# A decoder layer's merge moved from GpSimd and a shared PSUM bank to VectorE and the score banks, with three edits in its MLP

## The chip, the cores and the metric

The kernel runs on one core of one Trainium2 chip, as one program. The metric is the device time of one execution in microseconds (us); lower is better. Engines: PE (TensorE, matmuls), DVE (VectorE), ACT (ScalarE), POOL (GpSimd), SP (SyncE, which issues the DMAs). Each engine works through its own instructions in a fixed order.

## What is computed

One decoder layer on a prompt of 2048 tokens and a sample of 64 tokens (8 sequences of 8), all in float32:

```python
n = rms_norm(x, ln1_g); proj = n @ w_in                     # 1024 -> 3360 columns
att = dilated_attention(q, k, v, ...)                       # 8 heads x 64, three branches
rw  = rwkv7_time_mix(proj[..., 3 * A_W:], ...)              # recurrent half, 8 heads x 64
h = x + concat([att, rw]) @ w_out
m = rms_norm(h, ln2_g)
y = h + jnp.square(jax.nn.relu(m @ w_mlp1)) @ w_mlp2        # 1024 -> 4096 -> 1024
```

The attention has three branches, (window, dilation) = (128,1), (512,4), (2048,16). Each gives a numerator, a denominator and a row maximum, and the branches are merged with weights `exp(max - max over branches)` over the common denominator. The sample attends to a cache of 2048 keys.

## The kernel before

Products in float32 are split into a high and a low part (`parts` and `split`: ACT writes the high part, DVE or POOL subtracts it to get the low one), and three matmuls high*high, high*low, low*high are summed in PSUM. The program is written as generators; a scheduler that simulates the engines sets the final order on each engine, and memory of a closed pool is taken over by the next pool, whose tiles then wait for the last readers of what lay there.

The stages are, by time: projections and recurrence (0 to 1212 us), prompt attention (1212 to 1790), output projection beside the sample's attention (1790 to 1987), and the MLP (1987 to the end).

**Attention.** `attention(p, ...)` runs head pairs p = 0 to 3. Per pair there are 96 score tiles in three branches b: two matmuls into a score bank of pool `psc` (3 banks, tile `sc`, L1087 and L1088), a bias add with row maximum on DVE (L1090), an exponential on ACT, transposes into `pt` (L1105), and products with the values into `o` (L1112). ACT copies `o` into `ob[b]`. Tile `ob[0]` has two buffers, `ob[1]` and `ob[2]` have one each, so ACT's first copy for branch 1 of pair p+1 waits until pair p is merged. `merge(p, ob, st)` is pumped two steps at a time inside `attention(p+1)`; for p = 3 it runs beside the start of the sample. It makes small products of the maxima and denominators (L1135, L1136, L1144 to L1155), computes the weights on a [128, 128] tile, sends them through memory (`wD`) into the tile `wrow`, and then takes 12 steps, one for each group g of 512 tokens and branch b:

```python
ps = mp()
PE.matmul(ps, wsel[:, g], wr[:, b], start=True, stop=True)
tt(ob[b][:, cs], ps, ob[b][:, cs], ALU.mult)
if b:
    (V if p == 3 else G).tensor_tensor(ob[0][:, cs], ob[0][:, cs], ob[b][:, cs], ALU.add)
```

For p < 3 `mp()` gives the tile `ax` of pool `pax`, which has a single bank. The same bank serves `recurrent_half()`, also pumped inside the attention: 64 groups of 12 matmuls (L1263), each followed by a DVE add `fr`. For p = 3 it gives a score bank.

**MLP.** Three column groups g of 704 columns, 8 rounds r each. A round makes the first product for two blocks f with seven products each (Strassen, `first`, L1628), and then the second product (`second`, L1696) for eight row blocks o; in normal rounds the first part takes 168 matmuls and the second 192. In `second` the weight tile of each o is split by `parts(wr)`, high on ACT and low on DVE (L1571); in `first` products 2 and 6 of the seven have their low part on POOL. In the last round of groups 0 and 1 the generator `normed` builds the seven operand sets of the next group beside `second`: DVE scales (L1493, tile `rl`), POOL makes four sums (L1581 to L1584), ACT and DVE split them (`mh`, `ml`). In the first round of group 0 three operand sets (`quarter`) are still built on DVE and ACT while PE multiplies.

`square_sums` gives the RMS sums of 88 columns: two squares on ACT, three adds on DVE, a matmul with `ones` (L1465). Four of them are left for the end of round 0 of group 0. They read the tile `res1`, which `reload(1)`, at the end of round 1, fills again.

**Memory.** Pool `mw` (weight tiles `wr`, `wh`, `wl`, then `rl` and the squares) is opened after the output projection and starts at byte 110944 of a partition, where pool `wo2` lay: `wr` takes 110944 to 127328, and `wo2`, with the operand tiles `mh` and `ml` of the last projection matmuls, took 110944 to 125024.

Of the kernel before, what the change touches and what calls it, by code (L numbers as in the profile page):

```python
# [9 lines left out]
F32 = mybir.dt.float32  # L10
F32R = mybir.dt.float32r
AF = mybir.ActivationFunctionType
ALU = mybir.AluOpType
# [4 lines left out]
P = 128  # L18
# [12 lines left out]
def bc(ap, axis, n):  # L31
    a = ap.unsqueeze(axis)
    shape = list(a.shape)
    shape[axis] = n
    return a.broadcast_to(shape)
# [136 lines left out]
def _build(ctx, tc, nc, I, O, dbg, upto):  # L172
    V, S, PE, G = nc.vector, nc.scalar, nc.tensor, nc.gpsimd
# [7 lines left out]
    def tt(out, a, b, op):  # L181
        V.tensor_tensor(out, a, b, op)  # L182
# [4 lines left out]
    def pool(**kw):  # L187
        if kw.get("space") is not DRAM:
            kw["reuse_waits"] = "tile"
        return tc.tile_pool(**kw)  # L190
# [6 lines left out]
    ones = const.tile([P, P], F32, name="ones")  # L197
# [791 lines left out]
    psc = ph2.enter_context(pool(name="psc", bufs=3, space=PSUM, side="right"))  # L989
# [137 lines left out]
    def merge(p, ob, st):  # L1127


        def mp():  # L1130
            return psc.tile([P, 512], F32, name="sc") if p == 3 else pax.tile([P, 512], F32, name="ax")

        for ty in range(2):
            for x in range(2):
                G.tensor_tensor(zst[:, x, :, :, 4 * ty:4 * ty + 4], bc(st[:, x, 1, :, ty, :].rearrange("p g q -> p q g"), 3, 4), bc(bc(mk1, 1, 4), 1, 4), ALU.mult)  # L1135
                G.tensor_tensor(mv2[:, ty, x], bc(st[:, x, 2, :, ty, :], 3, 8), bc(bc(rr2, 1, 4), 1, 4), ALU.mult)  # L1136
            yield
        sw = at.tile([P, 6, P], F32, name="sw")
        ps = mp()
# [12 lines left out]
        ps = mp()  # L1152
# [43 lines left out]
        for g in range(4):  # L1196
            cs = slice(g * 512, (g + 1) * 512)
            for b in range(3):
                ps = mp()
                PE.matmul(ps, wsel[:, g], wr[:, b], start=True, stop=True)  # L1200
                tt(ob[b][:, cs], ps, ob[b][:, cs], ALU.mult)
                if b:
                    (V if p == 3 else G).tensor_tensor(ob[0][:, cs], ob[0][:, cs], ob[b][:, cs], ALU.add)
                yield
            nc.sync.dma_start(out=mixA[p, :, cs], in_=ob[0][:, cs])

# [246 lines left out]
    def residual(g):  # L1453
        return hp.tile([P, KT, 2 * HT], F32, name=f"res{g % 2}")

    def square_sums(h, i, c, ps, pl):

        sa = pl.tile([P, 4, SQ], F32, name="sq", tag="mt2", bufs=2)
        sb = pl.tile([P, 4, SQ], F32, name="sq", tag="mt2", bufs=2)
        act(sa, h[:, 0:4, c:c + SQ], AF.Square)  # L1460
        act(sb, h[:, 4:8, c:c + SQ], AF.Square)
        tt(sa, sa, sb, ALU.add)
        tt(sa[:, :2], sa[:, :2], sa[:, 2:], ALU.add)
        tt(sa[:, 0], sa[:, 0], sa[:, 1], ALU.add)
        PE.matmul(ps[:SQ, 0:1], sa[:, 0], ones[:, 0:1], start=True, stop=True)  # L1465
        V.tensor_copy(ssq[i // 8][:SQ, i % 8:i % 8 + 1], ps[:SQ, 0:1])
        if i % 8 == 7:
            q = ssq[i // 8]
            tsc(q, q, 1.0 / D, 1e-6, ALU.mult, ALU.add)
            G.tensor_tensor(rst[i // 8], q, mhalf[:, 0:8], ALU.pow)  # L1470
# [42 lines left out]
    with pool(name="wo2", bufs=1) as wo2, pool(name="pwo", bufs=4, space=PSUM, side="right") as pwo, pool(name="psa", bufs=1, space=PSUM) as psa, pool(name="pst", bufs=1, space=PSUM) as pst:  # L1513
        for k in range(4):
            wo_panel(kqb.tile([P, T], F32R, name="wo", tag="kq"), k)
        for _ in range(2):
            kvt = kqb.tile([P, T], F32, name="kv2", tag="kq")
            kvs += [lambda t=kvt[:, i:i + 1024]: t for i in (0, 1024)]
        sample = sample_all(psa)
        owed = 0  # L1520
        sums0 = sums_first(wo2, lambda: pst.tile([P, 512], F32, name="pst")[:, :HT], m0, rb0)
        for c0 in range(0, NT, NC_):
            if c0 + NC_ == NT:
                for _ in sample:
                    pass
            g, q0 = c0 // (2 * HT), c0 % (2 * HT)
            if q0 == 0:
                res = residual(min(g, 1))
                res0 = res0 if g else res
            h = res[:, :, q0:q0 + NC_]  # L1530
            nc.sync.dma_start(out=h, in_=rD[:, :, c0:c0 + NC_])
            for k in range(4):
                if (k, c0) not in mixed:
                    mixed[k, c0] = mix_panel(*((we, k, c0, 3) if k < 3 else (wo2, k, c0, 2)))
            for o in range(KT):
                ps = pwo.tile([P, 512], F32, name="pwo")
                i = 0
                for k in range(4):
                    mh, ml = mixed[k, c0]
                    for a, b in ((woh, mh), (woh, ml), (wol, mh)):  # L1540
                        PE.matmul(ps[:, :NC_], a[k][:, o * P:(o + 1) * P], b, start=(i == 0), stop=(i == 11))  # L1541
                        i += 1
                tt(h[:, o], ps[:, :NC_], h[:, o], ALU.add)
                if g and o % 4 == 2:
                    next(sums0, None)
                owed += 8
                while owed >= 5:
                    owed -= 5
                    next(sample, None)
            if g:  # L1550
                nc.sync.dma_start(out=hD[:, :, c0:c0 + NC_], in_=h)
            if c0 + NC_ < NT:
                for i in range(NC_ // SQ):
                    square_sums(h, c0 // SQ + i, i * SQ, pst.tile([P, 512], F32, name="pst"), wo2)
    ph3.close()
    mw = ph4.enter_context(pool(name="mw", bufs=2))


# [3 lines left out]
    with pool(name="mm", bufs=1, side="right") as mm, pool(name="pm", bufs=8, space=PSUM) as pm:  # L1562
# [21 lines left out]
            E.tensor_tensor(S[3], B21, S[1], ALU.subtract)  # L1584

        def tmp():
            return mw.tile([P, HT], F32, name="rl", bufs=12)

        def reload(g):
            h = residual(g)  # L1590
# [3 lines left out]
        def normed(g, h, mb):  # L1594

            mb += [operand(i, hp if i in EARLY else mm) for i in range(7)]
            rb = scales(g, mw, bank)
            yield
            for k in range(4):
                B11, B12, B21, B22 = (scaled(V, h, rb, k, x, c, tmp()) for x in range(2) for c in range(2))  # L1600
                S = [tmp() for _ in range(4)]
                sums_b(G, S, B11, B12, B21, B22)
                for i, t in enumerate((B11, B21, B22, *S)):
                    split(t, mb[i][0][:, k], mb[i][1][:, k])
                    if i == 2:
                        yield
                yield
# [76 lines left out]
        def second(r, hs, h, last, base, beside):  # L1684

            for o in range(KT):
                wr = mw.tile([P, 4, P], F32, name="wr", tag="wr", bufs=8)
                nc.sync.dma_start(out=wr, in_=I["w2"][r, o])
                wh, wl = parts(wr)
                for c in range(2):  # L1690
                    ps = bank()
                    cs = slice(c * HT, (c + 1) * HT)
# [11 lines left out]
        for g in range(3):  # L1704
            late = []
            nh = None
            for r in range(8):
# [11 lines left out]
                beside = normed(g + 1, nh, mb2) if last and g < 2 else iter(())  # L1719
                second(r, hs, h, last, g * 2 * HT, beside)  # L1720
                if g == 0 and r == 0:
                    for i in range(20, 24):
                        square_sums(res, i, (i - 16) * SQ, pm.tile([P, 512], F32, name="pm"), mw)
                if g < 2 and r == 1:
                    nh = reload(g + 1)
                for _ in beside:
                    pass
# [37 lines left out]
```

## Time and profile before

| what | us |
|---|---|
| median of 3 runs | 3433.43 |
| lowest, highest run | 3427.34, 3434.07 |
| the profiled execution, its own time | 3430.08 |
| its span, first to last instruction | 3428.3 |
| PE busy | 3165.2 (92%) |
| DVE busy | 2171.6 (63%) |
| ACT busy | 1465.3 (43%) |
| POOL busy | 1071.6 (31%) |
| mean granted clock of PE | 0.955 |

Busy time counts an engine's instructions; PE can be busy at half its clock. Idle time of the other engines costs nothing unless PE waits for them. The device time holds 1.8 us beside the span.

### The profile page before, as it was taken

How to read it: one execution, taken by the hardware profiler on the slowest of the kernel's cores; microseconds unless marked ns; L12 is line 12 of the kernel's file. 1: busy time of each engine (PE TensorE's matmuls, PEld its weight loads, DVE VectorE, ACT ScalarE, POOL GpSimd, SP SyncE). 2: the span in 40 equal slices, each digit the busy share in tenths (PEclk: the TensorE clock that was granted, in tenths of full speed). 3: DMA queues.
4: the chain of work that ended last, by engine and by line, in shares of the span. 5: the costliest groups of instructions: out<-in, count | busy, mean ns of one | idle time of the engine just before them, and what ended most of it. 6: DMA issues, size and time to landing. Idle time of an engine off the chain costs nothing.

```text
span 3428.3 us, 64759 instructions
## 1 busy us (share of the span) xinstructions
PE 3165.2 (92%) x24406; PEld 2883.9 (84%) x24406; DVE 2171.6 (63%) x4576; ACT 1465.3 (43%) x3468; POOL 1071.6 (31%) x1311
## 2 busy tenths in 40 slices
PE   5999999989988889897989789999999999999999
PEld 5877867887887878686868579999999999899999
DVE  4656686776675444353556666767776666967675
ACT  4555565555454356262532333323333333423232
POOL 1004431343044111323210133333543333534342
PEclk9999999999998999897989889999999999999999
DMA  5465575465455575343457722222232222322122
GB/s 165 136 193 153 132 202 151 115 164 161 129 152 134 162 230 170 93 153 98 113 198 262 288 82 93 87 62 87 70 128 71 75 74 75 105 62 87 62 87 71
DMA packets 374493, 439.73 MB, mean 128 GB/s; under 512 B 120067, under 2 KB 236734, under 8 KB 374180
## 3 DMA queue, kind: packets, MB, share of 16 engines
q1 hardware_dynamic: 374180, 435.59, 42.4%
q8 instruction: 192, 3.15, 0.4%
q14 instruction: 121, 0.99, 0.1%
HBM read 338.07 MB, written 102.11 MB: 128 GB/s over the span
## 4 chain that ended last, share of the span: by engine, by line
PE 71%; DVE 11%; DMA 9%; issue 3%; SPq 3%; POOL 2%; ACT 2%; DVEq 0%; ACTq 0%; POOLq 0%
PE pm L1696 20%; PE pm L1628 17%; PE pj L335 8%; PE pj L803 4%; PE ax L1263 3%; PE o L1112 3%; PE pwo L1541 3%; PE pt L1105 2%; PE sc L1087 2%; PE sc L1088 2%; DVE ml L182 1%; DMA wr<-in_wq 1%; DMA xg<-in_xg 1%; DVE rl L1493 1%; DVE ob L182 1%
## 5 line engine op out<-in xcount | busy, mean ns | idle before, releaser
L185 ACT ACTIVATE wh<-wr 128x512 fp32r<-128x512 f32 x744 | 463.4, 625 | 823.9 <-PE pm L1696 474.3
L1696 PE MATMUL pm<-fh,wl 128*128 128x352 f32 x1536 | 496.4, 323 | 8.6 <-DVE wl L1571 8.6
L1696 PE MATMUL pm<-fh,wh 128*128 128x352 f32 x1536 | 493.6, 324 | 0.0
L1696 PE MATMUL pm<-fl,wh 128*128 128x352 f32 x1536 | 492.7, 323 | 0.4 <-DVE fl L182 0.4
L1628 PE MATMUL pm<-mh,wh 128*128 128x352 f32 x1344 | 437.1, 326 | 13.8 <-ACT wh L185 11.7
L1628 PE MATMUL pm<-mh,wl 128*128 128x352 f32 x1344 | 433.9, 324 | 5.3 <-DVE wl L1571 5.3
L1628 PE MATMUL pm<-ml,wh 128*128 128x352 f32 x1344 | 434.5, 324 | 3.3 <-DVE ml L182 3.3
L182 DVE TENSOR_TENSOR res<-pm,res 128x352 f32<-128x352 f32 x384 | 198.4, 522 | 288.2 <-PE pm L1696 285.5
L1571 DVE TENSOR_TENSOR wl<-wr,wh 128x512 fp32r<-128x512 f32 x432 | 364.3, 843 | 12.9 <-ACT wh L185 10.0
L1696 PEld LDWEIGHTS pm<-fh,wl 128*128 128x128 f32 x1536 | 290.2, 189 | 9.6 <-DVE wl L1571 9.4
L1696 PEld LDWEIGHTS pm<-fl,wh 128*128 128x128 f32 x1536 | 289.3, 189 | 1.2 <-DVE fl L182 1.0
L1696 PEld LDWEIGHTS pm<-fh,wh 128*128 128x128 f32 x1536 | 289.4, 189 | 0.7 <-ACT fh L185 0.2
L1628 PEld LDWEIGHTS pm<-mh,wh 128*128 128x128 f32 x1344 | 254.9, 190 | 14.9 <-ACT wh L185 12.0
L1628 PEld LDWEIGHTS pm<-mh,wl 128*128 128x128 f32 x1344 | 254.4, 189 | 8.5 <-DVE wl L1571 8.4
L1628 PEld LDWEIGHTS pm<-ml,wh 128*128 128x128 f32 x1344 | 255.1, 190 | 5.0 <-DVE ml L182 4.9
L803 PE MATMUL pj<-wh,nh 128*128 128x256 f32 (+1 forms) x816 | 242.2, 298 | 9.6 <-ACT qn L185 7.3
L803 PE MATMUL pj<-wh,nl 128*128 128x256 f32 (+1 forms) x816 | 241.5, 296 | 5.0 <-DVE nl L182 4.8
L1575 POOL TENSOR_TENSOR wr<-wr 128x512 f32<-128x512 f32 x48 | 63.0, 1313 | 578.9 <-DVE wl L1571 470.2
L803 PE MATMUL pj<-wl,nh 128*128 128x256 f32 (+1 forms) x816 | 241.2, 296 | 0.1
L335 PE MATMUL pj<-nh,wh 128*128 128x512 f32 (+3 forms) x600 | 222.0, 373 | 20.3 <-ACT nh L185 10.2
L182 DVE TENSOR_TENSOR wl<-wr,wh 128x512 fp32r<-128x512 f32 (+1 forms) x216 | 149.9, 696 | 134.9 <-ACT wh L185 131.6
L1090 DVE CUSTOM_DVE_ANT_0 e<-sc,bt 128x256 f32<-128x256 f32 (+1 forms) x384 | 133.3, 363 | 147.5 <-PE sc L1088 111.3
(327 smaller groups left out, 7609.2 us busy)
## 6 DMA issues: line engine op xcount, KB each, us to landing
wr<-in_w SPq DMA_DIRECT2D x384, 256.0 KB
wr<-in_wr SPq DMA_DIRECT2D x120, 256.0 KB
wr<-in_wq SPq DMA_DIRECT2D x96, 256.0 KB
kv<-in_kc SPq DMA_DIRECT2D x40, 512.0 KB
kv<-in_vc SPq DMA_DIRECT2D x40, 512.0 KB
xsD<-xst SPq DMA_DIRECT2D x56, 256.0 KB
xrkv<-xsD SPq DMA_DIRECT2D x32, 384.0 KB
vt<-vD SPq DMA_DIRECT2D x48, 256.0 KB
```

The source lines that it names most:

```text
L182: V.tensor_tensor(out, a, b, op)
L185: S.activation(out, in_, func, bias=bias, scale=scale, **kw)
L335: PE.matmul(ps[:m, :n], a[:, k, :m], b[h * 4 + k][:, c0:c0 + n], start=(h == 0 and i == 0), stop=(h == 1 and i == 11))
L803: PE.matmul(out, a[h * 2 + k][:, i * P:i * P + m], b[:, k, :], start=(h == 0 and q == 0 and i % 2 == 0), stop=(h == 3 and q == 5 and (i % ...
L1087: PE.matmul(ps[:, c0:c0 + n], cols(qst, b, i, False), cols(kst, b, i, both), start=True, stop=False)
L1090: V.tensor_tensor_reduce(out=e[:, c0:c0 + n], in0=ps[:, c0:c0 + n], in1=bts[ty][:, bts[ty].shape[1] - n:], scale=-1.0, scalar=3e38, op0=AL ...
L1112: PE.matmul(o[ty * 64:ty * 64 + 64, (i % 4) * P:(i % 4 + 1) * P], kv[:, ty * 64:ty * 64 + 64], ptss[ty][:, y * P:(y + 1) * P], start=fst, ...
L1263: PE.matmul(ps[:, :FT], w[k][a][:, o * P:(o + 1) * P], m[k][b], start=(i == 0), stop=(i == 11))
L1541: PE.matmul(ps[:, :NC_], a[k][:, o * P:(o + 1) * P], b, start=(i == 0), stop=(i == 11))
L1571: (G if pooled else V).tensor_tensor(wl, w, wh.bitcast(F32), ALU.subtract)
L1628: PE.matmul(ps, a[:, k], b[:, k], start=(n == 0), stop=(n == 11))
L1696: PE.matmul(ps, a[:, f], b[:, cs], start=(i == 0), stop=(i == 11))
```

## The change

Four edits.

1. `merge`: every pair uses a score bank of `psc`, the small products of the maxima and denominators and the eight adds per merge go to DVE.
2. `square_sums` is cut in two: `squares` (ACT and DVE, result in a tile `sqs` of its own with four buffers) and the matmul with what follows. For the last four, `squares` stays at the end of round 0 of group 0, the matmuls go to the end of round 1, and `reload` moves from the end of round 1 to that of round 2.
3. In the last rounds of groups 0 and 1 the low weight parts of `second` are made on POOL.
4. A new pool `mt` takes `rl`, the squares and `dg2`, and is opened ahead of `mw`. Tiles `wr` now lie at 132064 to 148448, where the sample's tiles `sbias`, `qSs`, `pts`, `kSs`, `qbd` lay (131360 to 148352) and `wh`, `wl` at 148448 to 164832, over the sample's `attS`, `pr` and `kv`. Tile `rl` takes 112352 to 129248, over `wo2`.

```diff
         def mp():
-            return psc.tile([P, 512], F32, name="sc") if p == 3 else pax.tile([P, 512], F32, name="ax")
+            return psc.tile([P, 512], F32, name="sc")
...
-                G.tensor_tensor(zst[...], ..., ALU.mult)
-                G.tensor_tensor(mv2[:, ty, x], ..., ALU.mult)
+                V.tensor_tensor(zst[...], ..., ALU.mult)
+                V.tensor_tensor(mv2[:, ty, x], ..., ALU.mult)
...
-                    (V if p == 3 else G).tensor_tensor(ob[0][:, cs], ob[0][:, cs], ob[b][:, cs], ALU.add)
+                    V.tensor_tensor(ob[0][:, cs], ob[0][:, cs], ob[b][:, cs], ALU.add)
...
-    def square_sums(h, i, c, ps, pl):
+    def squares(h, c, pl):
...
-        tt(sa[:, 0], sa[:, 0], sa[:, 1], ALU.add)
-        PE.matmul(ps[:SQ, 0:1], sa[:, 0], ones[:, 0:1], start=True, stop=True)
+        q = hp.tile([P, SQ], F32, name="sqs", bufs=4)
+        tt(q, sa[:, 0], sa[:, 1], ALU.add)
+        return q
+
+    def square_sums(sq, i, ps):
+        PE.matmul(ps[:SQ, 0:1], sq, ones[:, 0:1], start=True, stop=True)
...
     ph3.close()
+    mt = ph4.enter_context(pool(name="mt", bufs=1))
     mw = ph4.enter_context(pool(name="mw", bufs=2))
...
-            return mw.tile([P, HT], F32, name="rl", bufs=12)
+            return mt.tile([P, HT], F32, name="rl", bufs=12)
...
-                wh, wl = parts(wr)
+                wh, wl = parts(wr, last and base < 4 * HT)
...
                 if g == 0 and r == 0:
-                    for i in range(20, 24):
-                        square_sums(res, i, (i - 16) * SQ, pm.tile([P, 512], F32, name="pm"), mw)
-                if g < 2 and r == 1:
+                    sqs = [squares(res, i * SQ, mt) for i in range(4, 8)]
+                if g == 0 and r == 1:
+                    for i in range(4):
+                        square_sums(sqs[i], 20 + i, pm.tile([P, 512], F32, name="pm"))
+                if g < 2 and r == 2:
                     nh = reload(g + 1)
```

What the scheduler makes of it shows in the order of the instructions. Up to the end of pair 0 the order is the same. First PE in the attention, at the first four merge matmuls (L1200) of pair 0, before:

```order
L1087 MATMUL sc<-kst_15352,qst_15354 128x128
L1088 MATMUL sc<-klo_15353,qst_15354 128x128
L1200 MATMUL ax<-wrow,wsel 128x512 x4
L1263 MATMUL ax<-fmh,fwh_14872 128x264
L1263 MATMUL ax<-fml,fwh_14872 128x264
L1263 MATMUL ax<-fmh,fwl_14873 128x264
```

and now:

```order
L1263 MATMUL ax<-fmh,fwh_14882 128x264
L1200 MATMUL sc<-wrow,wsel 128x512 x2
L1087 MATMUL sc<-kst_15352,qst_15354 128x256
L1088 MATMUL sc<-klo_15353,qst_15354 128x256
L1263 MATMUL ax<-fml,fwh_14882 128x264
L1263 MATMUL ax<-fmh,fwl_14883 128x264
L1087 MATMUL sc<-kst_15355,qst_15357 128x256
L1088 MATMUL sc<-klo_15356,qst_15357 128x256
L1263 MATMUL ax<-fmh,fwh_14934 128x264
L1200 MATMUL sc<-wrow,wsel 128x512
```

Before, all 12 merge matmuls stand behind the score matmuls of pair 1 that fit, with only recurrent groups between them; now they stand between scores of branch 0. Counted over DVE's and ACT's listings: DVE's 12 multiplications of that merge stood behind score 168 of the whole attention and now lie between scores 116 and 138; ACT's first copy into the `ob[1]` of pair 1 stood behind exponential 168 and now stands behind exponential 139. Pairs 1 and 2 look alike (212 to 234 against 234, 308 to 330 against 332).

Between the last of the products of the maxima (L1155) and the first merge matmul PE had 87, 59 and 146 other matmuls for pairs 0, 1 and 2, and has 123, 73 and 131 now.

Second, SP's queue at the start of the MLP (`wr<-in_w` are its weights, `hD<-res` stores the last part of h, L1615 and L1622 are the same line), before:

```order
L1329 DMA kv_20905<-in_vc 128x1024
L1327 DMA kv_20905<-vSD 8x512
L1615 DMA wr<-in_w 128x512 x2
L1551 DMA hD<-res_22538 1024x1x352
L1615 DMA wr<-in_w 128x512 x6
```

and now:

```order
L1327 DMA kv_20905<-vSD 8x512
L1622 DMA wr<-in_w 128x512 x8
L1556 DMA hD<-res_22554 1024x1x352
L1695 DMA wr<-in_w 128x512 x4
L1598 DMA res_25083<-hD 128x8x704
L1695 DMA wr<-in_w 128x512 x4
```

The weights of the first two blocks stand ahead of the last store, right behind the sample's last load; the reload of `res1` stands between two halves of the first `second`'s weights.

Third, POOL at the end of group 0 (L1571 and L1578 make a low weight part, L1581 to L1584 and L1588 to L1591 are the sums of `normed`), before:

```order
L1571 TENSOR_TENSOR wl<-wr,wh 128x512 x2
L1639 TENSOR_TENSOR rl<-rl 128x352 x2
L1581 TENSOR_TENSOR rl<-rl 128x352
L1582 TENSOR_TENSOR rl<-rl 128x352
L1583 TENSOR_TENSOR rl<-rl 128x352
L1584 TENSOR_TENSOR rl<-rl 128x352
```

and now:

```order
L1578 TENSOR_TENSOR wl<-wr,wh 128x512 x4
L1646 TENSOR_TENSOR rl<-rl 128x352
L1578 TENSOR_TENSOR wl<-wr,wh 128x512
L1646 TENSOR_TENSOR rl<-rl 128x352
L1578 TENSOR_TENSOR wl<-wr,wh 128x512
L1588 TENSOR_TENSOR rl<-rl 128x352
L1589 TENSOR_TENSOR rl<-rl 128x352
L1590 TENSOR_TENSOR rl<-rl 128x352
L1591 TENSOR_TENSOR rl<-rl 128x352
L1578 TENSOR_TENSOR wl<-wr,wh 128x512 x2
```

Four of the eight parts (two more belong to `first`) come ahead of the sums, the rest among them.

## Rows read from the trace of the kernel before

**Rows 1.** Page, first part: busy time, share of the span and instructions of each engine.

```profile
PE 3165.2 (92%) x24406; PEld 2883.9 (84%) x24406; DVE 2171.6 (63%) x4576; ACT 1465.3 (43%) x3468; POOL 1071.6 (31%) x1311
```

**Rows 2.** Waits of ACT from 1212 to 1790 us (the attention): who waited for whom, us in total, times, longest.

```profile
ACT ob L185 <- POOL ob L1203: 92.7, 3, 40.9
```

**Rows 3.** ACT in order of time: start, length, instruction, and in brackets the idle time before it with its releaser. Two of the copies that waited.

```profile
1436.85 1.08 ACT L185 ACTIVATE ob<-o 128x512 f32<-128x512 f32 x2 [37.45 <-POOL ob L1203]
...
1586.90 1.08 ACT L185 ACTIVATE ob<-o 128x512 f32<-128x512 f32 x2 [40.88 <-POOL ob L1203]
```

**Rows 4.** PE in order of time at the start of the first of these waits: the first two merge matmuls, and the first matmul of a recurrent group behind them.

```profile
1404.66 0.77 PE L1200 MATMUL ax<-wrow,wsel 128*128 128x512 f32 x1 [5.05 <-DMA wrow<-wD]
1406.21 0.80 PE L1200 MATMUL ax<-wrow,wsel 128*128 128x512 f32 x1 [0.78 <-DVE ob L182]
...
1411.04 0.56 PE L1263 MATMUL ax<-fmh,fwh 128*128 128x264 f32 x1 [0.87 <-DVE ob L182]
```

**Rows 5.** Busy time by stretch: length, then busy us (and instructions) of PE, PEld, DVE, ACT, POOL, granted PE clock, DMA share, GB/s. First an undisturbed stretch of the attention, then those of the three waits.

```profile
1300.00:1399.60 99.60, 99.60 (x826) 88.11 (x825) 52.26 (x222) 58.84 (x205) 18.70 (x36) 1.00 0.48 154
1399.60:1438.80 39.20, 22.36 (x69) 15.28 (x68) 10.03 (x16) 1.08 (x2) 16.41 (x20) 0.60 0.27 83
1545.60:1588.00 42.40, 22.28 (x63) 15.05 (x64) 10.73 (x18) 1.50 (x3) 17.12 (x22) 0.52 0.26 81
1705.60:1722.90 17.30, 12.10 (x42) 8.93 (x41) 4.33 (x7) 1.09 (x2) 7.91 (x8) 0.60 0.34 108
```

**Rows 6.** By line: count, then min/median/max ns, first and last start. L1200 and L1203 of the merge; behind them one recurrent group from the chain that ended last (start, us, what), and two instructions of the chain of the merge's weights on ACT.

```profile
L1200 PE MATMUL ax<-wrow,wsel x36: 416/793/797, 1404.7 to 1718.4; 128*128 128x512 f32 x36
L1203 POOL TENSOR_TENSOR ob<-ob,ob x24: 1266/1273/1290, 1407.8 to 1720.1; 128x512 f32<-128x512 f32 x24
L1203 DVE TENSOR_TENSOR ob<-ob,ob x8: 679/682/692, 1779.8 to 1792.9; 128x512 f32<-128x512 f32 x8
L1136 POOL TENSOR_TENSOR mv<-st,mcon x16: 403/408/792, 1314.4 to 1755.6; 128x128 f32<-128x128 f32 x16
...
1365.52 1.46 PE ax L1263 x12
...
1386.85 0.36 ACT L185 ACTIVATE sw<-ax 128x256 f32<-128x256 f32 x1
```

**Rows 7.** Waits of PE from 1212 to 1790 us, those of pairs 0 to 2 for the merge's weights: us in total, times, longest.

```profile
PE ax L1200 <- DMA wrow<-wD: 13.4, 2, 8.3
```

**Rows 8.** Busy time by stretch in the MLP, columns as in rows 5: the first part of the first round, and the last second products of group 0 and of group 1.

```profile
1987.00:2037.20 50.20, 33.71 (x170) 31.32 (x170) 38.90 (x55) 21.36 (x44) 22.70 (x16) 0.80 0.37 115
2448.80:2507.80 59.00, 50.66 (x286) 48.21 (x284) 58.07 (x87) 25.51 (x52) 37.77 (x28) 0.94 0.32 108
2922.00:2976.40 54.40, 48.24 (x271) 45.59 (x269) 54.27 (x82) 22.42 (x47) 31.00 (x25) 0.94 0.24 84
```

**Rows 9.** The chain that ended last, in order of time: start, us, what. The second product of the first round, the first part of the second round, and that of the third.

```profile
2037.22 30.92 PE pm L1696 x192
...
2076.59 28.28 PE pm L1628 x168
...
2135.48 26.72 PE pm L1628 x168
```

**Rows 10.** The start of the MLP in order of time, PE and POOL, and with them the sample's last read of `attS` on ACT; behind them SP's wait there (us in total, times, longest).

```profile
1998.70 0.66 PE L1628 MATMUL pm<-mh,wh 128*128 128x352 f32 x1 [11.67 <-ACT wh L185]
...
1996.72 1.26 POOL L1575 TENSOR_TENSOR wr<-wr 128x512 f32<-128x512 f32 x1 [71.60 <-DMA wr<-in_w]
...
1969.51 0.69 ACT L185 ACTIVATE mh<-attS 128x64 fp32r<-128x64 f32 x4 [0.84 <-DVE attS L1350]
...
SPq L1615 <- PE pwo L1541: 16.5, 1, 16.5
```

**Rows 11.** DVE in order of time: the first low weight parts of the MLP, and the adds of two of the square sums.

```profile
1998.68 1.20 DVE L1571 TENSOR_TENSOR wl<-wr,wh 128x512 fp32r<-128x512 f32 x1 [9.34 <-ACT wh L185]
2000.03 3.22 DVE L1571 TENSOR_TENSOR wl<-wr,wh 128x512 fp32r<-128x512 f32 x2
...
2072.34 1.19 DVE L182 TENSOR_TENSOR sq<-sq 128x352 f32<-128x352 f32 x3 [0.38 <-ACT sq L185]
```

**Rows 12.** PE in order of time: the long waits in the last rounds of groups 0 and 1.

```profile
2475.14 0.43 PE L1696 MATMUL pm<-fh,wl 128*128 128x352 f32 x1 [1.72 <-DVE wl L1571]
2481.89 0.43 PE L1696 MATMUL pm<-fh,wl 128*128 128x352 f32 x1 [2.65 <-DVE wl L1571]
...
2951.03 0.66 PE L1696 MATMUL pm<-fh,wl 128*128 128x352 f32 x1 [4.20 <-DVE wl L1571]
```

**Rows 13.** Low weight parts by engine (as rows 6): on DVE in the second product of group 0's last round, on POOL from 2100 us on. Behind them two stretches of DVE (`ml`) with what POOL did during the first.

```profile
L1571 DVE TENSOR_TENSOR wl<-wr,wh x7: 672/679/1346, 2448.3 to 2484.7; 128x512 fp32r<-128x512 f32 x7
L1571 POOL TENSOR_TENSOR wl<-wr,wh x88: 1286/1408/1744, 2138.0 to 3386.9; 128x512 fp32r<-128x512 f32 x88
...
2468.03 2.80 DVE L182 TENSOR_TENSOR ml<-rl,mh 128x352 fp32r<-128x352 f32 x2
2471.18 1.38 DVE L182 TENSOR_TENSOR ml<-rl,mh 128x352 fp32r<-128x352 f32 x3
...
2467.51 1.40 POOL L1584 TENSOR_TENSOR rl<-rl 128x352 f32<-128x352 f32 x1
2468.88 1.57 POOL L1576 TENSOR_TENSOR wr<-wr 128x512 f32<-128x512 f32 x1
```

More of the change, by code (lines that the diff above doesn't have):

```diff
@@ L1130, in mp @@
         def mp():
-            return psc.tile([P, 512], F32, name="sc") if p == 3 else pax.tile([P, 512], F32, name="ax")
+            return psc.tile([P, 512], F32, name="sc")
         for ty in range(2):
             for x in range(2):
-                G.tensor_tensor(zst[:, x, :, :, 4 * ty:4 * ty + 4], bc(st[:, x, 1, :, ty, :].rearrange("p g q -> p q g"), 3, 4), bc(bc(mk1, 1, 4), 1, 4), ALU.mult)
-                G.tensor_tensor(mv2[:, ty, x], bc(st[:, x, 2, :, ty, :], 3, 8), bc(bc(rr2, 1, 4), 1, 4), ALU.mult)
+                V.tensor_tensor(zst[:, x, :, :, 4 * ty:4 * ty + 4], bc(st[:, x, 1, :, ty, :].rearrange("p g q -> p q g"), 3, 4), bc(bc(mk1, 1, 4), 1, 4), ALU.mult)
+                V.tensor_tensor(mv2[:, ty, x], bc(st[:, x, 2, :, ty, :], 3, 8), bc(bc(rr2, 1, 4), 1, 4), ALU.mult)
             yield
@@ L1553, in _build @@
                 for i in range(NC_ // SQ):
-                    square_sums(h, c0 // SQ + i, i * SQ, pst.tile([P, 512], F32, name="pst"), wo2)
+                    square_sums(squares(h, i * SQ, wo2), c0 // SQ + i, pst.tile([P, 512], F32, name="pst"))
     ph3.close()
+    mt = ph4.enter_context(pool(name="mt", bufs=1))
     mw = ph4.enter_context(pool(name="mw", bufs=2))
@@ L1596, in normed @@
             mb += [operand(i, hp if i in EARLY else mm) for i in range(7)]
-            rb = scales(g, mw, bank)
+            rb = scales(g, mt, bank)
             yield
```

## The prediction

> **What bounds the kernel now.** I read the page's first part first: PE is busy for 92% of the span, every other engine for 63% or less [rows 1]. So only time in which PE stands still, or runs at the low clock, can be won here, and the question for each edit is which idle stretch of PE it closes. The waits lead to them. In the attention ACT waited three times, 92.7 us in all, for POOL's add into `ob` [rows 2], twice for 37.45 and 40.88 us in one piece [rows 3]. The reader should see that this is not harmless waiting of an idle engine: ACT makes the exponentials too, its queue is in order, and behind the blocked copy no score tile is finished. The table by stretch shows what PE did meanwhile: in 100 undisturbed us 826 matmuls at clock 1.00 and no idle time, in the three stretches of 39.2, 42.4 and 17.3 us only 69, 63 and 42 at clock 0.52 to 0.60 [rows 5]. What there was to do came in steps through the one bank `ax`: the second merge matmul starts 1.55 us after the first and waited 0.78 us for DVE's multiplication [rows 4]; at the unhalved clock such a matmul takes 0.42 [rows 6].
>
> In the MLP I followed PE's waits in order of time: 11.67 us ahead of the first product [rows 10], a gap between 2068.14, where the first round's second product ends, and 2076.59 [rows 9], and waits for DVE's low weight parts of 1.72, 2.65 and 4.20 us in the last rounds of groups 0 and 1 [rows 12]. There DVE is busy for 58.07 of 59.0 and 54.27 of 54.4 us [rows 8]: in those stretches it, not PE, is the bound.
>
> **The change part by part.** All sums are against the profiled execution, 3430.08 us, 3.4 below the median of the runs shown and inside their spread of 6.7.
>
> *Merge, the stretches of waiting.* Useful work in the three stretches: the first two hold 12 merge matmuls each, the third five; the rest (57, 51, 37) are mostly recurrent, 1.46 us per 12 [rows 5, 6]. That is 12 x 0.42 + 57 x 0.122 = 12.0, then 11.2 and 6.6, together 29.8 of 98.9 us. So 69 us are the most that can come back. With the score banks a step no longer waits for the bank of the step before, and the steps stand among scores of branch 0; ACT's copy now stands behind about as many exponentials as the merge needs score tiles, some 30 earlier than where it used to block, and with an order that has put the merge ahead of it I expect it to wait little.
>
> What remains is the chain that makes the weights. In pairs 0 and 1 PE has 87 and 59 other matmuls between the last product of the maxima and the first merge matmul. By the undisturbed stretch one is worth 99.60 / 826 = 0.121 us [rows 5], so 10.5 and 7.1 us, and with the waits for `wrow`, 13.4 us in two, of which the first was 5.05 [rows 4, 7], both come to 15.5 us. That is how long these weights take from there. Now 123, 73 and 131 matmuls stand there, 14.8, 8.8 and 15.8 us, which leaves 0.7, 6.7 and 0 open, together 7.4. The products ahead of it (behind the last exponentials and maxima of the pair, which PE has just produced) and clock lost in these holes I put at 3.5 us per merge, an estimate from the 0.87 and 0.78 us that one PE-DVE hand-over costs here [rows 4], four of them. Residue 7.4 + 10.5 = 18; gain 51, rounded down to **50**. Bounds: 69 if all is hidden, 20 if the whole stretch from `sw` (1386.85) to the first merge matmul (1404.66), 17.8 us, stays open in all three merges less what scores fill, i.e. 16 each [rows 4, 6].
>
> *Merge, what DVE gets.* 24 adds of 0.68 us, which took POOL 1.27 [rows 6], and per merge a few small products, on POOL 0.40 each [rows 6]; at the same price 4 to 12 of them are 2 to 5 us. Some 8 us per merge over 30 to 40 us, beside a DVE that is busy 52 of 100 us there [rows 5]: I cost it at nothing. If that cover were gone, the price is the second rival below.
>
> *Start of the MLP.* SP issued the weights 16.5 us late, after the last matmul of the output projection, since they land where its operands lie; POOL waited 71.60 us for them [rows 10]. Now they land where the sample's tiles lay, last read at 1969.51 [rows 10], some 18 us ahead, and the issue stands ahead of the store of h. So the 11.67 us go. But not all of it counts, for the first part is then bound by DVE: 38.9 of 50.2 us from 1987 on [rows 8], nearly all of it behind 1998.7. What DVE can do ahead of 1987 are the first three low parts, 1.20 + 3.22 = 4.4 us [rows 11]; what it gets in addition are squares that used to lie in the gap, three adds of 1.19 a pair [rows 11], some 3 to 4 us. So the end of the first part moves from 2037.2 to about 2027: **10**. Bounds: 0 (DVE gains nothing), 16 (11.67 + 4.4). The reload of `res1`, moved a round later and issued between two halves of the first `second`'s weights, waits for the squares and the store of h; the weights behind it are needed 15 us later (four of eight row blocks, 30.92 / 8 = 3.9 us each [rows 9]), which covers it. If not, the weights are late by about what the transfer takes, a few us.
>
> *Square sums.* The gap of 8.45 us goes, since the matmuls stand a round later, when the squares have long been made; and the first part behind it took 28.28 instead of 26.72 at the full clock, 1.56 more [rows 9]. Four matmuls with their hand-overs remain, 0.5. Gain **9.5**, bounds 5 (a hand-over with DVE for each stays, 4 x 0.87, and the slow start) and 10.
>
> *Last rounds.* Eight low parts per transition leave DVE, 0.68 each by the median, 1.35 at most [rows 13]; with 0.85 as a mean between beside-POOL and alone 6.8 us per transition. POOL gets 8 x 1.41 = 11.3 [rows 13], of 38 and 31 busy in 59 and 54 [rows 8], so it has the time. But it slows DVE: two splits `ml` took 2.80 us while POOL ran for 1.40 + 1.57 = 2.97 us, three took 1.38 without it [rows 13]. That is 2.80 - 0.92 = 1.88 lost in 2.97, 0.63 per us of POOL. With some 0.8 of DVE's work there of that kind: 11.3 x 0.8 x 0.63 = 5.7 lost, 6.8 won, 1.1 per transition, **2** in both. Bounds: 8.6 (all three waits [rows 12] go) and -9 (each of POOL's parts costs DVE its whole length, 11.3 - 6.8 = 4.5 per transition). The Trainium skill, "SBUF — State Buffer", section "Who interferes with whom", says that a DVE instruction with two SBUF inputs and a GpSimd instruction that reads SBUF hold their shared port in turn, one fully shut out by the other. By that the term would be -9; the trace's 0.63 is part of that only.
>
> Sum: 50 + 10 + 9.5 + 2 = 71.5, so 3430.1 - 71.5 = **3359 us**.
>
> **The rivals.**
>
> *The stall becomes PE's.* PE is in order as well; where it comes to the first merge matmul before `wrow` has landed it stands, with all scores behind it. For it: 8.3 us of such a wait are there already [rows 7], and DVE's small products now queue behind maxima in the same chain. Against it: more matmuls now stand in front in two of the three merges. If the chain gets 10 us longer each time, 30 of the 50 are lost: 3389 us.
>
> *DVE as the new bound, slower.* The steps now stand among scores in PE's and DVE's queues and take score banks. If DVE is late and each step is exposed, one costs 1.57 us for the hand-over as before, 0.68 for the add and 0.87 until DVE comes to it [rows 4, 6], 3.1 us; 36 of them are 112 us against the 69 that were lost. Then 3430 + 43 - 21.5 = 3452 us. It decides from 2.5 us a step, (69 + 21.5) / 36. Against it: PE idle nothing and DVE half idle in the undisturbed stretch [rows 5].
>
> *DVE shut out by POOL in the last rounds.* The -9 above in place of 2: 3370 us. For it the 2.80 [rows 13]; against it that two splits still went through in 2.97 us of POOL.
>
> *The weights come no earlier in effect*, because DVE's work sets the end of the first part whatever its start: 0 in place of 10, 3369 us. For it DVE's 38.9 us [rows 8].
>
> **How the numbers follow.** My forecast 0.62; the stall at PE 0.18; POOL's shutting out 0.08; no earlier start 0.08; slower through DVE 0.04. A measurement of this kernel tells about 0.2%, 7 us, from no change. All but the last rival are faster by far more: faster 0.95, same 0.01, slower 0.04. The range goes from 3330 (merges at their upper bound, start and transitions near theirs: 69 + 14 + 10 + 7 = 100) to 3394 (the first rival with a few us less on the transitions); outside lie the last rival and the far ends.
>
> **What would show it.** Right: ACT's waits for `ob` all but gone; merge matmuls on `sc` among scores, no stretch of the attention at clock 0.6 longer than 10 us; attention ended near 1740 instead of 1790; the first L1628 straight behind the output projection; no 8 us hole behind the first second product, four short L1465 a round later; DVE without low parts in the last rounds, and PE's waits there on `rl` and `ml`. Wrong: waits of PE for `wrow` over 10 us, DVE nearly full during merges, PE waiting for POOL's `wl` or for weights behind the reload, or `ml` and `rl` of 1.4 us throughout.

## The result, and the profile after

The changed kernel takes 3372.28 us (median of 4 runs, 3366.30 to 3376.55) against 3431.92 before: ratio 0.9827, interval 0.9808 to 0.9845, so 60 us less. The forecast was 3359 with a range of 3330 to 3394. The profiled execution took 3373.22 us.

The page's first part, that answers to [rows 1]:

```profile
span 3371.4 us, 64724 instructions
PE 3141.7 (93%) x24406; PEld 2869.0 (85%) x24406; DVE 2183.4 (65%) x4616; ACT 1462.4 (43%) x3468; POOL 1057.1 (31%) x1271
```

The work is the same, 24406 matmuls: 57 us of span went, 24 us of them PE's busy time (matmuls that had run at the low clock) and 33 us of standing still. To see where, I cut both traces at the same matmuls. L1087 are the scores, L1541 the output projection and L1696 the second products, by the line numbers of the kernel before:

| stretch, cut at PE's matmuls | before | after | gained | forecast |
|---|---|---|---|---|
| start to the first score L1087 | 1217.6 | 1222.0 | -4.4 | 0 |
| first score to first output projection L1541 | 574.1 | 524.4 | 49.7 | 50 |
| first to last output projection | 195.0 | 199.1 | -4.1 | 0 |
| last output projection to first L1696 | 50.4 | 36.4 | 14.0 | 10 |
| first L1696 to that of the third round | 125.0 | 115.8 | 9.2 | 9.5 |
| first L1696 of group 0's last round to first of group 1 | 72.0 | 74.5 | -2.5 | 1 |
| the same, group 1 to 2 | 69.7 | 74.8 | -5.1 | 1 |

The last two rows are called the first and the second transition below. All other stretches agree within 0.5 us. The first row is nothing of the change: up to there the order is the same, and in the traces of all kernels below it lies between 1213.4 and 1224.7.

**Attention.** From 1212 to 1750 us, ACT's waits for `ob`, and PE's for the merge's weights (us in total, times, longest), for [rows 2, 7]:

```profile
ACT ob L185 <- PE o L1112: 27.5, 31, 3.0
```

```profile
PE sc L1200 <- DMA wrow<-wD: 12.1, 4, 5.4
```

The releaser POOL is gone, and what is left are 31 short waits for the products themselves, 3.0 us the longest. The time has not turned into a wait of PE for the weights: 12.1 us in four merges. PE in order of time at the first merge matmuls of pairs 0, 1 and 2:

```profile
1357.25 1.19 PE L1200 MATMUL sc<-wrow,wsel 128*128 128x512 f32 x2 [2.58 <-DMA wrow<-wD]
...
1487.15 1.19 PE L1200 MATMUL sc<-wrow,wsel 128*128 128x512 f32 x2 [5.36 <-DMA wrow<-wD]
...
1618.28 1.11 PE L1200 MATMUL sc<-wrow,wsel 128*128 128x512 f32 x2 [3.24 <-DMA wrow<-wD]
```

Two now run back to back where they were 1.55 us apart [rows 4]. The table by stretch (columns of [rows 5]) over the three merges:

```profile
1354.00:1388.00 34.00, 31.38 (x229) 29.05 (x230) 24.59 (x76) 14.63 (x51) 7.90 (x13) 0.90 0.46 137
1484.00:1519.00 35.00, 31.71 (x204) 27.99 (x205) 24.78 (x74) 14.80 (x51) 12.53 (x22) 0.85 0.43 131
1615.00:1652.00 37.00, 32.18 (x232) 29.01 (x232) 25.74 (x79) 16.31 (x54) 6.44 (x11) 0.95 0.68 186
```

Stretches of 34 to 37 us hold over 200 matmuls where those of 39.2 and 42.4 us held 69 and 63, DVE is at 70% or a little more with its new work, and the granted clock is 0.85 to 0.95 instead of 0.52 to 0.60.

**Start of the MLP.** PE and DVE in order of time, for [rows 10, 11]: the last output projection matmul, the first of the MLP, and the first low weight parts.

```profile
1945.50 0.33 PE L1546 MATMUL pwo<-mh,wo 128*128 128x352 f32 x1
1945.66 0.32 PE L1635 MATMUL pm<-mh,wh 128*128 128x352 f32 x1
...
1937.30 0.85 DVE L1578 TENSOR_TENSOR wl<-wr,wh 128x512 fp32r<-128x512 f32 x1
1938.60 1.26 DVE L1578 TENSOR_TENSOR wl<-wr,wh 128x512 fp32r<-128x512 f32 x1
1940.52 1.04 DVE L1578 TENSOR_TENSOR wl<-wr,wh 128x512 fp32r<-128x512 f32 x1
```

The three parts are made between the output projection's adds, 8 us ahead of use, and no hole is left. By stretch, the first part of the first round, its second product, the next first part, and the next second product with the square sums' matmuls ([rows 8, 9]):

```profile
1945.70:1981.90 36.20, 30.34 (x169) 29.07 (x168) 34.57 (x58) 19.45 (x42) 15.63 (x11) 0.91 0.45 153
...
1981.90:2012.90 31.00, 31.00 (x195) 30.61 (x194) 22.20 (x39) 7.66 (x14) 9.10 (x6) 1.00 0.30 98
2012.90:2039.60 26.70, 26.70 (x170) 26.70 (x170) 21.28 (x31) 12.76 (x24) 15.44 (x12) 1.00 0.32 94
2039.60:2070.80 31.20, 31.20 (x202) 31.19 (x200) 17.84 (x31) 6.61 (x11) 6.25 (x5) 1.00 0.18 56
```

DVE fills 34.57 of the 36.2 us, so it is most likely still the bound there; the gap of 8.45 us behind is gone, PE is full at clock 1.00, and the square sums' matmuls (eight instructions for the four products) cost 0.6 us a round later.

**Last rounds.** Both transitions by stretch, first in the kernel before, then in the changed one:

```profile
2448.70:2520.70 72.00, 63.66 (x366) 61.21 (x366) 70.10 (x107) 31.75 (x64) 44.00 (x32) 0.95 0.40 139
2921.90:2991.60 69.70, 63.52 (x367) 60.84 (x366) 68.65 (x102) 30.73 (x63) 39.31 (x32) 0.95 0.29 96
...
2384.50:2459.00 74.50, 63.95 (x366) 61.03 (x365) 72.38 (x100) 30.72 (x64) 50.99 (x38) 0.91 0.39 134
2860.30:2935.20 74.90, 65.48 (x367) 61.99 (x366) 70.62 (x98) 31.24 (x64) 49.58 (x38) 0.91 0.30 93
```

DVE has fewer instructions (100 for 107, 98 for 102) and is busy longer. The reason can be seen in the rows of the two engines from one stretch of the first transition, DVE first, then POOL:

```profile
2396.84 5.88 DVE L1498 SCALAR_TENSOR_TENSOR rl<-res,ln,rb 128x352 f32<-128x352 f32 x4
2402.64 1.28 DVE L182 TENSOR_TENSOR ml<-rl,mh 128x352 fp32r<-128x352 f32 x1
2403.84 0.51 DVE L182 TENSOR_TENSOR res<-pm,res 128x352 f32<-128x352 f32 x1
2404.27 3.91 DVE L182 TENSOR_TENSOR ml<-rl,mh 128x352 fp32r<-128x352 f32 x3
2408.11 0.51 DVE L182 TENSOR_TENSOR res<-pm,res 128x352 f32<-128x352 f32 x1
2408.54 2.36 DVE L182 TENSOR_TENSOR ml<-rl,mh 128x352 fp32r<-128x352 f32 x2
...
2397.69 3.11 POOL L1578 TENSOR_TENSOR wl<-wr,wh 128x512 fp32r<-128x512 f32 x2
2400.76 1.57 POOL L1582 TENSOR_TENSOR wr<-wr 128x512 f32<-128x512 f32 x1
2402.30 1.23 POOL L1588 TENSOR_TENSOR rl<-rl 128x352 f32<-128x352 f32 x1
2403.49 1.59 POOL L1583 TENSOR_TENSOR wr<-wr 128x512 f32<-128x512 f32 x1
2405.03 1.58 POOL L1578 TENSOR_TENSOR wl<-wr,wh 128x512 fp32r<-128x512 f32 x1
2406.57 1.22 POOL L1589 TENSOR_TENSOR rl<-rl 128x352 f32<-128x352 f32 x1
2407.77 1.22 POOL L1590 TENSOR_TENSOR rl<-rl 128x352 f32<-128x352 f32 x1
2408.95 1.57 POOL L1584 TENSOR_TENSOR wr<-wr 128x512 f32<-128x512 f32 x1
```

POOL works without a pause, and DVE gets through about one instruction with two operands in SBUF per POOL instruction: 1.2 to 1.5 us for each `rl` and `ml`, on the average of a row, which take 0.57 (at 2390.18 in this trace) and 0.46 [rows 13] alone. The adds `res`, one operand of which is in PSUM, stay at 0.51.

### The profile page after: what moved, and what is told of

Same layout as the page of the kernel before. It is cut to its first block, busy times and chain, and to the rows that moved or that the text cites. A ratio compares the mean times of both kernels' runs of the same rounds, so it can differ in the third digit from the quotient of the medians.

```text
span 3371.4 us, 64724 instructions
## 1 busy us (share of the span) xinstructions
PE 3141.7 (93%) x24406; PEld 2869.0 (85%) x24406; DVE 2183.4 (65%) x4616; ACT 1462.4 (43%) x3468; POOL 1057.1 (31%) x1271
## 5 line engine op out<-in xcount | busy, mean ns | idle before, releaser
L1578 DVE TENSOR_TENSOR wl<-wr,wh 128x512 fp32r<-128x512 f32 x416 | 348.6, 838 | 3.5 <-ACT wh L185 0.6
L185 ACT ACTIVATE e<-e,st 128x256 f32<-128x256 f32 (+1 forms) x384 | 174.9, 456 | 136.5 <-DVE st L1090 133.8
```

The costliest lines, as they stand in the source:

```text
L185: S.activation(out, in_, func, bias=bias, scale=scale, **kw)
L1578: (G if pooled else V).tensor_tensor(wl, w, wh.bitcast(F32), ALU.subtract)
```

## The experiments

Theory: the merge's time was held by the single bank and the order that followed from it; the start by the place of the weights; and in the last rounds VectorE loses to GpSimd's low parts more than it is spared. Rivals: GpSimd's slowness in the merge, VectorE's work at the start, and lateness or order in the last rounds. The stretches named below are those of the first table.

**Bank alone, engines alone.** Two kernels from the one before:

```diff
 merge_bank
-            return psc.tile([P, 512], F32, name="sc") if p == 3 else pax.tile([P, 512], F32, name="ax")
+            return psc.tile([P, 512], F32, name="sc")
 merge_dve
-  G.tensor_tensor(zst[...   G.tensor_tensor(mv2[...   (V if p == 3 else G).tensor_tensor(ob[0]...
+  V.tensor_tensor(zst[...   V.tensor_tensor(mv2[...   V.tensor_tensor(ob[0]...
```

> The kernel before with the score banks for every merge, and nothing else: adds and small products stay on GpSimd. Theory (the single bank was the bound: it made steps of 1.57 us and kept the merge behind the scores): first score matmul to first output projection matmul, 574 us before and 524 after, comes to 525 to 535, ACT waits for ob under 20 us, total 3382 to 3392 us. Rival (GpSimd's adds held ACT): under 10 us of the 50 come, 3422 us or more.

> The kernel before with the adds and small products of the merge on VectorE, the single bank kept. Theory (bank): the 1.55 us pitch of the merge matmuls stays, and with it ACT's waits for ob (then released by VectorE), gain 0 to 10 us, 3422 to 3432. Rival (GpSimd): 40 us or more come, 3392 or less.

The bank alone: 3383.47 us, ratio 0.9851 (0.9831 to 0.9872), attention 517.7 us, shorter than expected and than the changed kernel's 524.4. The engines alone: 3434.31 us, ratio 1.0001 (0.9986 to 1.0015), attention 577.1. ACT's wait and PE's pitch of the latter kernel:

```profile
ACT ob L185 <- DVE ob L1203: 90.7, 3, 41.1
```

```profile
1406.03 0.77 PE L1200 MATMUL ax<-wrow,wsel 128*128 128x512 f32 x1 [5.01 <-DMA wrow<-wD]
1407.58 0.80 PE L1200 MATMUL ax<-wrow,wsel 128*128 128x512 f32 x1 [0.79 <-DVE ob L182]
```

The releaser's name changed from POOL to DVE and the 92.7 us became 90.7. So the engine that a wait names was not its cause: the bank was, with the order that the scheduler makes of it (no run separates these two). Taking the merge off GpSimd, by itself, is worth nothing.

**The engines, with the score banks.** Four kernels with edits 1, 2 and 4 and without 3, on one chip; adds and small products each on VectorE or GpSimd (`both_dve` is the kernel dve_parts below).

> The kernel dve_parts once more, beside the next three on one chip: adds and small products of the merge on VectorE. Attention 524 us, as in its first profile.

> The same with only the merge's small products back on GpSimd. Theory (they stand in the chain to the weights and are held up behind maxima on VectorE): attention 517 to 519 us, waits of PE for wrow 3 to 5 us in place of 12. Rival (the adds fill VectorE at the wrong time): 523 to 525.

> The same as both_dve with only the adds back on GpSimd. Theory (products): 523 to 525 us, waits for wrow about 12. Rival (adds): 517 to 519.

> The kernel best once more: both on GpSimd, score banks. Attention 516 to 518 us in the profile; if the 7 us are real, its median is 5 to 8 us under that of both_dve on this chip. Rival (given back later, in the output projection beside the sample, which took 202.3 us in its first profile and 193 to 198 in those with the late merge): medians within 3 us of each other.

| kernel | median us | ratio, interval | attention | output projection | sum |
|---|---|---|---|---|---|
| both_dve | 3361.16 | 0.9793, 0.9780 to 0.9807 | 525.7 | 198.2 | 723.9 |
| prods_pool | 3373.60 | 0.9824, 0.9808 to 0.9840 | 526.2 | 206.2 | 732.4 |
| adds_pool | 3363.06 | 0.9800, 0.9786 to 0.9814 | 507.9 | 213.0 | 720.9 |
| both_pool | 3367.39 | 0.9806, 0.9787 to 0.9826 | 513.2 | 207.1 | 720.3 |

My theory of the small products fell: with them alone on GpSimd the attention stayed at 526 us. With the adds alone there it shows 508, the opposite of what I wrote, but this figure can't be compared with the others. There the scheduler set the first output projection matmul, at which I cut, 142 matmuls earlier in PE's order, so work moved from the one stretch to the other. PE's count in the output projection shows it, adds_pool first, then both_pool (columns of [rows 5]):

```profile
1732.60:1945.60 213.00, 179.73 (x1750) 148.12 (x1750) 128.49 (x397) 61.24 (x138) 29.28 (x23) 0.85 0.73 264
...
1727.50:1934.60 207.10, 171.64 (x1608) 142.02 (x1609) 126.17 (x378) 60.49 (x137) 29.39 (x23) 0.86 0.72 250
```

In all other kernels each of the two stretches holds as many matmuls as before. Between those PE's waits differ, and most of all one near the end of the attention, for the sample's cache, whose scores (L1298) begin there. From 1212 to 1750 us, both_dve first, then both_pool:

```profile
PE sc L1298 <- DMA kv<-in_kc: 11.6, 6, 8.8
...
PE sc L1298 <- DMA kv<-in_kc: 1.9, 3, 0.8
```

One wait of 7.6 to 8.9 us is in every trace with the score banks and the adds on VectorE, the changed kernel's too, and in none with the adds on GpSimd. (The waits for `wrow` are 12.5 us in both_dve and 5.2 in both_pool.) In both_pool the output projection is 8.9 us longer than in both_dve, which gives most of the 12.5 back. The sum of the two stretches is 723.5 to 732.4 us in the six traces with score banks and the adds on VectorE, and 717.9 to 720.9 in the five with the adds on GpSimd (merge_bank, best and best_early with them). The medians do not show these 2.6 us or more: both_pool's is higher than both_dve's. That kernel ran twice (as best, below), and both times its profiled execution was the fastest of its runs by 11 us (3355.83 of 3355.83 to 3371.93 here), so its stretches look better than it is; that of adds_pool was the slowest of its runs. By the medians the adds' engine makes no difference that these runs can tell, and the highest, prods_pool, lies clear of both_dve alone. What decides the sum of the two stretches stays open.

> The kernel dve_parts with the merge's adds and small products back on GpSimd, the score banks kept. Theory (the products on VectorE lengthen the chain to the weights): attention 518 us in place of 524, ACT's waits for ob still under 5 us, total 3358. Rival (the 6 us came from something else in the kernel before): 524, 3365.

That was its first run, on another chip than dve_parts: 3367.47 us, ratio 0.9797 (0.9777 to 0.9818), attention 516.3, output projection 202.3. The attention came as expected, the total of 3358 did not.

**Memory alone**: the kernel before with pool `mt` opened ahead of `mw`.

```diff
+    mt = ph4.enter_context(pool(name="mt", bufs=1))
     mw = ph4.enter_context(pool(name="mw", bufs=2))
...  mw.tile([P, HT], F32, name="rl"...), scales(g, mw, ...), square_sums(..., mw)  ->  mt
```

> The kernel before with the new pool for rl, squares and dg2 ahead of the weight tiles, nothing else. Theory (the weights' place in memory makes the late start): last output projection matmul to the first second product takes 36 to 40 us in place of 50, the gap of 8.4 us behind that product stays, 3418 to 3422. Rival (VectorE sets the end of the first part whatever its start): 46 to 50 us, 3428 to 3432.

3417.92 us, ratio 0.9954 (0.9937 to 0.9971). The start takes 34.6 us in place of 50.4, the first L1696 to that of the second round 69.8 (67.7 before), with the gap. The place is the cause, as expected; the gap behind the product stays without the split of the squares.

**Low parts back on VectorE**, the changed kernel without edit 3:

```diff
-                wh, wl = parts(wr, last and base < 4 * HT)
+                wh, wl = parts(wr)
```

> The changed kernel with the last rounds' low weight parts back on VectorE. Theory (each GpSimd part costs VectorE about as much as it saves or more, since the two take turns at memory): last second product to next group's second product takes 72 and 70 us as before, in place of 74.5 and 74.9, so 3364 us, 8 less than the changed kernel. Rival (the parts on GpSimd pay, the loss there is from the new memory or order): 75 or more each, 3372 to 3380.

3364.96 us, ratio 0.9797 (0.9778 to 0.9815), and 3361.16 on the chip of the table above. The transitions take 72.4 and 69.7 us, as before:

```profile
2391.00:2463.40 72.40, 63.65 (x369) 61.33 (x369) 70.49 (x106) 31.50 (x65) 44.27 (x32) 0.95 0.41 138
2864.70:2934.40 69.70, 62.45 (x365) 59.38 (x363) 67.84 (x100) 30.18 (x63) 40.55 (x32) 0.98 0.30 99
```

DVE by line in the first of them (busy us, mean ns behind the bar), this kernel first, then the changed one:

```profile
L182 DVE TENSOR_TENSOR ml<-rl,mh 128x352 fp32r<-128x352 f32 x28 | 23.1, 850 | 0.9 <-ACT mh L185 0.9
L1578 DVE TENSOR_TENSOR wl<-wr,wh 128x512 fp32r<-128x512 f32 x18 | 16.1, 896 | 0.0
L1498 DVE SCALAR_TENSOR_TENSOR rl<-res,ln,rb 128x352 f32<-128x352 f32 x16 | 10.8, 707 | 0.0
```

```profile
L182 DVE TENSOR_TENSOR ml<-rl,mh 128x352 fp32r<-128x352 f32 x28 | 26.4, 974 | 0.0
L1498 DVE SCALAR_TENSOR_TENSOR rl<-res,ln,rb 128x352 f32<-128x352 f32 x16 | 13.8, 913 | 0.0
L1578 DVE TENSOR_TENSOR wl<-wr,wh 128x512 fp32r<-128x512 f32 x12 | 11.9, 996 | 0.1
```

Six parts left and saved 4.2 us; the same 28 `ml` and 16 `rl` cost 3.3 and 3.0 more, a balance of 2.1 us. That it equals the whole difference of the stretch, 74.5 against 72.4, is partly chance, since smaller lines moved too; but DVE, which fills the stretch but for 2 us in both kernels, is busy for 72.38 us instead of 70.49, and that is nearly all of it. In the second transition the same lines give 17.2 to 10.4 for the parts, 4.6 and 2.5 more for the others, 0.3 in sum, of 5.1 us lost. There the granted clock fell from 0.98 to 0.91, and DVE stood idle 4.3 us instead of 1.9, nearly all of it in waits for POOL's sums `rl` (L1646). So waiting for POOL is a part of that loss, and the rest is not accounted for.

**GpSimd work that nobody needs**, on the kernel dve_parts:

```diff
+                if last and base < 4 * HT:
+                    dm = mt.tile([P, 4, P], F32, name="dm", bufs=2)
+                    G.tensor_tensor(dm, wr, wr, ALU.subtract)     # dummy_read
+                    G.memset(dm, 0.0)                             # dummy_fill
```

> The kernel dve_parts with one more GpSimd instruction per row block in the two last rounds (eight each), which reads a weight tile twice and writes a tile that nobody reads. Theory (VectorE and GpSimd take turns at memory, 0.6 us of VectorE per us of GpSimd): 8 x 1.4 x 0.6 = 6.7 us on each transition, 72.4 and 69.7 become 79 and 76, total 3378. Rival (the loss in the changed kernel came from GpSimd being late or from the order): 72 to 74 and 70 to 72, 3365 to 3369.

> The same with a fill (memset) of the tile in place of the subtraction: GpSimd writes memory and reads none. Theory (they share the reading side): transitions of 72 to 73 and 70 to 71, 3365. Rival (any GpSimd instruction at work slows VectorE): as with the reads, or by 0.6 us per us of the fills.

3386.94 us and 3376.86 (ratios 0.9864, 0.9849 to 0.9879, and 0.9829, 0.9813 to 0.9846). Neither is what I meant. Nothing holds the fills back, and the scheduler put all 16 at 1919 us: they say nothing on reading and writing, which stays untried. Both kernels also lost 13 us at the start (49.8 and 49.5 us instead of 36.5). The tile `dm` moves the weight tiles 4096 bytes on, the order changes from there on, and now POOL's first instruction for the MLP stands behind the square sums, as its row in dummy_fill shows, some 8 us behind the last output projection matmul:

```profile
1954.32 1.55 POOL L1582 TENSOR_TENSOR wr<-wr 128x512 f32<-128x512 f32 x1 [27.75 <-DVE sq L182]
```

So dummy_fill is a control with the same layout and no GpSimd work there: transitions of 72.0 and 69.7. Against it the 16 readers, 21.4 us of POOL, mostly in the end of the last first part, cost 2.9 and 3.3 us in the transitions, 2.2 in the stretch between them and 1.0 in the one before, 9.4 in all, 0.44 per us of POOL, and the medians differ by 10.1. Nobody waits for their result, though GpSimd's own later instructions stand behind them, and the order of DVE's instructions around them is not quite the same in the two kernels. Shown is that more work on GpSimd costs time there, at less than the expected 0.6; by which path, VectorE's losses, GpSimd's lateness or the order, this run does not tell. The rows of dve_parts above speak for VectorE's losses in the first transition.

**Work ahead of the last round**, the kernel best with `scales` and the first quarter's scales and sums called before the last first part, `rl` with 17 buffers in place of 12:

> The kernel best with the scales and the first quarter of the next group's sums and operands put ahead of the last round's first part, in five more rl buffers. Theory (VectorE bounds the transitions, so its work there counts nearly one to one, and the first part has room for it): 4 x 0.57 + 2 x 0.5 us and four of GpSimd's sums leave, 4 to 6 us per transition, 67 and 65, total 3348 to 3352. Rival (the bound is the wait for the operand buffers, free only after the last first part): 70 to 72 each, 3357.

3384.66 us, ratio 0.9853 (0.9838 to 0.9868). The transitions take 73.5 and 73.9, not less, the stretches ahead of them 2.6 us more each, and the start again 50.2. The layout of memory moved too, so it does not tell which part of the edit costs what; as an improvement it failed.

## Why the prediction held, and where it failed

- *Merge, 50 forecast, 49.7 measured.* That the bank paced the merge, and that the chain of the weights would remain, was read rightly; that the number is met to 0.3 us is in part luck. The residual waits for `wrow` came to 11.2 us in the three merges, where I had 7.4 from the matmuls counted in front; added up they pass the 10 us that I had named as a sign of being wrong. The clock in the holes was 0.85 to 0.95. The 10.5 us for hand-overs were not measured. DVE's new work, which I put at nothing, comes in these traces with the 8.0 us wait for the sample's cache inside the attention, where the bank alone had gained 56.4 us; whether the work costs anything in the total stays open. Not foreseen: 4.1 us more in the output projection beside the sample. PE's 1607 matmuls of that stretch kept it busy for 172.0 us instead of 169.3, at a granted clock of 0.88 instead of 0.90. In the five traces in which PE's order up to the end of this stretch is that of the changed kernel it takes 198.2 to 201.0 us, in the two with the order of the kernel before 193.2 and 195.0 (in merge_dve, whose merge is as late, 198.0). So a part of the merge's gain seems to be given back there; why is not shown.
- *Start, 10 forecast, 14.0 measured.* The step was right: the place of the weights made the late start (mem_only). The term was too small. The added squares cost DVE 4.2 us, near the 3 to 4 forecast, but its busy time in the stretch fell from 38.90 to 34.57 nevertheless: the weight parts fell from 12.2 to 6.9, more than the 4.4 counted, and other lines moved both ways (twelve `ml` from 8.6 to 5.7, twelve `rl` from 9.1 to 11.1).
- *Square sums, 9.5 forecast, 9.2 measured.*
- *Last rounds, 2 forecast, -7.6 measured: the step that failed.* I charged 0.63 of DVE's time per us of POOL to 0.8 of its work, and credited 0.85 us for each of 16 parts. Against dve_parts, six parts left in the first transition, not eight (others are made ahead of it), at 0.70 each; the loss on `ml` and `rl` was 6.3 us for 6.7 us more POOL (44.27 to 50.99), 0.9 per us. One pair of rows [rows 13] with two splits in 2.97 us of POOL had already shown the same turn-taking, one DVE instruction per POOL instruction; I read it as a mean over a share of the work. The Trainium skill, "SBUF — State Buffer", section "Who interferes with whom", says that the shared port shuts the second engine out fully, and excepts DVE instructions with at most one SBUF input, outside DVE's two-port modes. The trace agrees in the first transition: 0.51 us for `res` throughout, and 1.2 to 1.5 for the others while POOL runs without a pause (I had named 1.4 us for `ml` and `rl` as a sign). By that rule the term was -9, nearer than mine; that it also fits the second transition's 5.1 us is not shown, since there a part came from waiting for POOL.
- The rivals: the stall did not become PE's (12.1 us in all); the start did come earlier; DVE as the new bound of the merge did not show. POOL shutting DVE out, given 0.08, is what happened in the first of the last rounds, and its 3370 us lies nearer to 3372.28 than my 3359; the other terms kept the total in range.

So the sum 71.5 became 56.9 of span: 9.6 less by the last rounds, 8.5 by the stretch before the scores, which varies between runs, and the output projection, and 3.4 more from the rest, mostly the start.

Fastest measured is the change without its third edit, 3361 to 3365 us, with adds_pool's 3363 not to be told from it: the 7 to 11 us that separate it from the changed kernel are near the 7.2 us of the two transitions, though the runs were not on one chip.

## What to carry to other kernels

A wait names the instruction that ended it, not the resource that set its time: here the engine alone left 91 of 93 us under another name, and the buffer that paced the chain removed them. Moving an elementwise instruction from a full VectorE to GpSimd did not pay here, where most of what remained on VectorE read two operands from SBUF; count its neighbours' losses, row by row, beside its own saving. Two stretches cut at the same matmul are comparable only if as many matmuls lie in them; count them first. Where weights are to be loaded early, look at what lay in their place and at which queue entry stands ahead of their first use; three kernels with some KB more in the pool ahead of the weights, and another order from there on, lost 13 us here.

## What had not been expected

In the rows above one VectorE instruction passed per GpSimd instruction while both read SBUF, whatever their own lengths: ten with two SBUF operands from 2396.84 to 2410.90, beside nine of GpSimd's that began in that time and one already under way. And with one order of instructions, the time to the first score matmul spread over 11 us, and the output projection over nearly 5 (202.3 and 207.1 in the two traces of one kernel), from one execution to the next: single profiles of this kernel tell a stretch's change only where the stretch itself repeats, as those of the MLP do within 0.5 us.
